# Second layer's modulation: from matmuls in PEER's query loop to GpSimd and ScalarE in the first FFN

## The chip, the cores and the metric

One core of a Trainium2 chip runs the whole kernel. The time is the device time of one execution in microseconds (us); every execution reads its weights from device memory. The engines have the names of the profile: PE (TensorE's matmuls), PEld (its weight loads), DVE (VectorE), ACT (ScalarE), POOL (GpSimd) and SP (SyncE, which here issues most of the loads).

## The reference, cut to what matters

The model is one block with mixers and a PEER layer (product keys and experts), then two layers of a diffusion-style transformer. T = 512 tokens, D = 1024, 256 context tokens, FFN width 22 x 128 = 2816.

```
def second_block(x, c, ctx, c_ctx, w_mod, b_mod, g_attn, g_ffn, ...):
    silu_c = jax.nn.silu(c)
    silu_cc = jax.nn.silu(c_ctx)
    for i in range(2):
        last = i == 1
        mod = silu_c @ w_mod[i] + b_mod[i]          # (1, 6 * 1024)
        mod_c = silu_cc @ w_mod[i] + b_mod[i]
        sh1, sc1, gt1, sh2, sc2, gt2 = jnp.split(mod[:, None, :], 6, axis=-1)
        ...
        h = modulate(rmsnorm(x, g_attn[i]), sh1, sc1)
        hc = modulate(rmsnorm(ctx, g_attn[i]), sh1c, sc1c)
        ...                                          # attention: neighbourhood (0), window (1)
        h = modulate(rmsnorm(x, g_ffn[i]), sh2, sc2)
        x = x + gt2 * conv_ffn(h, ...)
        if not last:
            hc = modulate(rmsnorm(ctx, g_ffn[i]), sh2c, sc2c)
            ctx = ctx + gt2c * conv_ffn(hc, ...)
    return x
```

The change concerns `mod` and `mod_c` of layer 1. They depend on the inputs alone, so they may be computed at any place before layer 1's attention. Of `mod_c` layer 1 uses only the shift and scale of the attention, 2048 of 6144 columns.

## The kernel before, in words

Activations lie transposed (features on partitions). A weight block of 512 KB is loaded by SP's queue (`wload`, three buffers `wraw`) and cut by `split_into` into two parts of a shorter format: ACT writes the high part (`wh`, line 183), DVE the rest (`wl`, line 184); four pairs are kept. PE multiplies three of the four products (lines 206 to 208). The instructions of each engine run in the order in which the build places them, which the engine's own list (the "order" below) shows; waits between engines are semaphores.

In front of the PEER layer's expert loop stand two stages. The query loop has 16 units (8 heads, 2 halves): a unit projects `acc` with `w_query`, copies it (`pq`), takes scores `sc` against the keys (line 863) and DVE searches the 16 largest of each row (`v`, line 843). Two generators are advanced in each unit: `fill(1 + half)` runs steps of `modulation` for layer 1 and `ahead(4)` runs steps of `early_products`, plain f32 matmuls of the first expert blocks (line 814, eight steps for an expert, 28 experts, 224 steps in all). The gate stage ("g_hot") is a pipeline of 96 items on DVE, ACT, POOL and PE (`eb`, `o`, `gps`); in each item `ahead(1 + ...)` runs what is left of the early steps.

`modulation` holds one PSUM bank: 3 groups x 8 blocks x 2 halves load `mraw` (512 KB each) and multiply it with `silc`, the silu of c and c_ctx (line 392).

The first FFN (`conv_ffn(0, True)`) has 11 groups of two j. `up` computes for each j a gate and a value block for the latents (128x512) and the context (128x256): matmuls to `acc`, the convolution on DVE (`cg`, `ca`, lines 1203 to 1205), a silu on ACT (line 1210), the product (line 1215) and its split (`fxh`, `fxl`, `fch`, `fcl`); it also splits the two blocks of `ffn_down` (`fwh`, `fwl`). `down` of the group before runs behind it: matmuls to `pd` (four banks), drained by DVE into XT and CT (line 1254).

`t2` is a pool of five buffers of 128x512 f32. A multiply of that shape on POOL exists in the attention before the FFN (`bias`, line 1355).

Of the kernel before, what the change touches and what calls it, by code (L numbers as in the profile page):

```python
# [10 lines left out]
F32 = mybir.dt.float32  # L11
# [10 lines left out]
D = 1024  # L22
# [85 lines left out]
def body(ctx: ExitStack, tc: tile.TileContext, a: dict, out: bass.AP, dbg=None, stop=None):  # L108
# [10 lines left out]
    def pool(stack, name, bufs=1, **kw):  # L119
        return stack.enter_context(tc.tile_pool(name=name, bufs=bufs, **kw))  # L120
# [256 lines left out]

    tables()

    def modulation(mp_, pmod, ly):  # L380

        bm = cload(mp_, "bmod", [128, 2, 48])
        for g in range(3):
            ps = pmod.tile([128, 512], F32, name="mod")
            for k in range(KT):
                for hf in range(2):

                    raw = mp_.tile([128, 4, 256], F32, name="mraw", bufs=2)
                    sy.dma_start(raw, a["w_mod"][ly, g, k, hf])
                    for c in range(4):  # L390
                        o = 32 * c
                        pe.matmul(ps[o:o + 32, hf * 256:hf * 256 + 256], sc[:, k], raw[:, c],  # L392
                                  start=k == 0 and hf == 0, stop=k == KT - 1 and hf == 1, tile_position=(0, o))
                if k < KT - 1:
                    yield
            rows = mp_.tile([128, 512], F32, name="mrow")
            se.activation(rows, ps, AF.Copy)
            tp = pmod.tile([128, 4, 128], F32, name="mod")
            for b_ in range(4):
                transpose(tp[:, b_], rows[:, b_ * 128:(b_ + 1) * 128])  # L400
            tv = tp.rearrange("p b (c r) -> p c b r", c=4)
            s = slice(g * 16, g * 16 + 16)
            bv = bm[:, ly, s].rearrange("p (c b) -> p c b", c=4)
            for dst, r_ in ((modx, 0), (modc, 1)):
                ve.tensor_tensor(dst[:, ly, s].rearrange("p (c b) -> p c b", c=4), tv[:, :, :, r_], bv, OP.add)
            yield
        for m_, gm in ((modx, gmx), (modc, gmc)):
            for i in range(2):
                ve.scalar_tensor_tensor(gm[:, ly, i * 8:i * 8 + 8], m_[:, ly, i * 24 + 8:i * 24 + 16], 1.0,
                                        c2[:, ly, i * 8:i * 8 + 8], OP.add, OP.mult)  # L410

    def fill(n=1):
        for _ in range(n):
# [355 lines left out]
    with ExitStack() as ex:  # L769
        ep = pool(ex, "peer")  # L770
        pp = ex.enter_context(ExitStack())
        pmod = pool(pp, "pmod", 1, space=PS)
        ph["mix"] = pool(pp, "pmixp", 4, space=PS)
        hh, hl = split_tile("h"), split_tile("l")

        xdr1 = dp.tile([KT, 128, T], F32, name="xdr1")
# [55 lines left out]
                next(early, None)  # L832

        with ExitStack() as gx:
            mp_ = pool(gx, "mod")
            kp_ = pool(gx, "topk")
            ph["mod"] = modulation(mp_, pmod, 1)
            v16 = kp_.tile([128, 4, 16, 16], F32, name="v16")
            i16 = kp_.tile([128, 4, 16, 16], U32, name="i16")
            vc = kp_.tile([128, 4, 8, 16], F32, name="vc")  # L840

            def top16(vals, idx, src, n, tag):
                ve.max(vals[:, 0:8], src)
                ve.max_index(idx[:, 0:8], vals[:, 0:8], src)
                rest = kp_.tile([128, n], F32, name="rest" + tag, bufs=2)
                ve.match_replace(rest, vals[:, 0:8], src, -3.4e38)
                ve.max(vals[:, 8:16], rest)
                ve.max_index(idx[:, 8:16], vals[:, 8:16], rest)

            for hd in range(8):  # L850
                for half in range(2):
                    u = hd * 2 + half
                    keys = kp_.tile([128, 128], F32, name="keys", bufs=2)
                    gp.dma_start(keys, a["keys"][u])
                    ps = acc()
                    proj(ps, wunit(a["w_query"][u]), h)
                    fill(1 + half)
                    ahead(4)
                    q = t2(name="pq")
                    se.activation(q, ps, AF.Copy)  # L860
                    st = mix([128, 4, 128], "sc")
                    for t in range(4):
                        pe.matmul(st[:, t], q[:, t * 128:(t + 1) * 128], keys, start=True, stop=True)
                    for t in range(4):
                        top16(v16[:, t, u], i16[:, t, u], st[:, t], 128, "k")
                for t in range(4):


                    cand = kp_.tile([128, 112], F32, name="cand", bufs=2)
                    for c0, i0, i1, nj in ((0, 0, 4, 16), (64, 4, 16, 4)):  # L870
                        gp.tensor_tensor(cand[:, c0:c0 + (i1 - i0) * nj].rearrange("p (a b) -> p a b", b=nj),
                                         v16[:, t, 2 * hd, i0:i1].unsqueeze(2).to_broadcast([128, i1 - i0, nj]),
                                         v16[:, t, 2 * hd + 1, 0:nj].unsqueeze(1).to_broadcast([128, i1 - i0, nj]), OP.add)
                    top16(vc[:, t, hd], ic[:, t, hd], cand, 112, "c")


            for t in range(4):
                ve.tensor_tensor(vc[:, t, :, 1:], vc[:, t, :, 1:], vc[:, t, :, 0:1].to_broadcast([128, 8, 15]),
                                 OP.subtract)
                ve.memset(vc[:, t, :, 0:1], 0.0)  # L880
            gate = kp_.tile([128, 4, 8, 16], F32, name="gate")
            se.activation(gate, vc, AF.Exp)
            gs = sm.tile([128, 4, 8], F32, name="gs", bufs=1)
            ve.tensor_reduce(gs, gate, AX.X, OP.add)
            ve.reciprocal(gs, gs)
            for t in range(4):
                ve.tensor_tensor(gate[:, t], gate[:, t], gs[:, t].unsqueeze(2).to_broadcast([128, 8, 16]), OP.mult)
            for t in range(4):
                if t == TS:
                    ve.tensor_copy(sgate, gate[:, t].rearrange("p h k -> p (h k)"))  # L890
                else:
                    tps = mix([128, 128], "gtp")
                    transpose(tps, gate[:, t].rearrange("p h k -> p (h k)"))
                    ve.tensor_copy(gT[:, t * 128:(t + 1) * 128], tps)
                ve.tensor_copy(ib16[:, t], i16[:, t])

            htok = rp.tile([128, D], F32, name="tok")
            for i in range(2):
                tps = mix([128, 4, 128], "htp")
                for k in range(4):  # L900
                    transpose(tps[:, k], hf[:, i * 4 + k, ND:])
                se.activation(htok[:, i * 512:i * 512 + 512], tps.rearrange("p k n -> p (k n)"), AF.Copy)
            fill(25)

        with ExitStack() as gx:
            gk = pool(gx, "ghot")
# [68 lines left out]
            def g_sum(it):  # L975
                it["ps"] = mix([128, 4, 128], "gps")
                for ti in range(4):
                    pe.matmul(it["ps"][:, ti], it["o2"][:, ti], it["o1"][:, ti], start=True, stop=True)  # L978
                ahead(1 + (it["q"] % 6 == 5))

            def g_out(it):
                th, tg = it["th"], it["tg"]
# [205 lines left out]
    def conv_ffn(ly, ctx_too):  # L1188
        with ExitStack() as fx:
# [2 lines left out]
            ft = pool(fx, "ft", 6)  # L1192
            ph["acc"] = pool(fx, "facc", 4, space=PS)
            ph["mix"] = pool(fx, "fmix", 4, space=PS)
            cv = cload(fp, "ffn_conv%d" % ly, [128, 4, 44])
            h = normed_x(ly, 1)
            hc = normed_c(fp, ly, 1) if ctx_too else None
# [20 lines left out]
            def up(grp):  # L1218
# [11 lines left out]
                for j in js:  # L1230
                    gs_ = {}
                    for half in (22, 0):
                        u = begun[half + j][0] if begun else wunit(a["ffn_up"][ly, half + j])
                        for i in range(1 if begun else 0, len(parts)):
                            hx, n, tg = parts[i][:3]
                            ps = acc(n=n)
                            proj(ps, u, hx)
                            if half:
                                gs_[i] = gate(ps, n, j)
                            else:  # L1240
                                ys[i].append(gated(ps, n, j, gs_[i], tg))
                        if half and ly == 0 and j == NJ - 1:
                            tables()
                    raw = wload(a["ffn_down"][ly, j], [128, KT, 128])
                    wd.append(split(raw, [128, KT, 128], fw, "fw", 4))
                return ys, wd
# [472 lines left out]
def layout(i):  # L1719
# [32 lines left out]
    for l in range(2):  # L1752
# [7 lines left out]
    o["bmod"] = np.ascontiguousarray(np.stack([colv(i["b_mod_2"][l]) for l in range(2)], 1))  # L1760

    o["w_mod"] = np.ascontiguousarray(
        i["w_mod_2"].reshape(2, KT, 128, 3, 4, 2, 256).transpose(0, 3, 1, 5, 2, 4, 6)).reshape(2, 3, KT, 2, 128, 1024)
    o["ctxT"] = np.ascontiguousarray(i["ctx_2"][0].T)
    o["na_qkv"] = chunks(i["na_w_qkv_2"][0], 256)
    o["na_o"] = units(i["na_w_o_2"][0])
# [31 lines left out]
```

## Time and profile before

| | us |
|---|---|
| median of 3 runs | 3405.89 (3403.52 to 3408.29) |
| profiled execution: time / span | 3405.12 / 3403.4 |
| PE busy | 3278.4 (96%) |
| DVE busy | 2352.6 (69%) |
| ACT busy | 1239.5 (36%) |
| POOL busy | 680.9 (20%) |
| query loop, about | 376 to 558 |
| gate stage, about | 558 to 780 |
| first FFN without its norms, about | 2216 to 2742 |

The span is the profiler's, from the first instruction to the last; the execution's own time is 1.7 us longer. Busy shares are means over stages with different limits, so each stage is read by itself. PE's busy time includes its pipelined ends; a share of 96% says only that PE is rarely without work.

### The profile page before, as it was taken

The numbers are of one execution on the slowest core, as the hardware profiler recorded it, in microseconds if no ns is written. First come the engines' busy times: TensorE is split into PE (matmuls) and PEld (weight loads), VectorE is DVE, ScalarE is ACT, GpSimd is POOL, SyncE is SP. The second block draws the span as 40 slices with busy tenths as digits, with TensorE's granted clock in tenths as the row PEclk, the third lists the DMA queues.
The fourth block names the chain that finished last, engine by engine and source line by source line (L and its number), as shares of the span: only waits on it lengthen the run. The fifth ranks groups of instructions, "written<-read, shape, count | busy, mean of one in ns | idle before, by whom it ended". The sixth has DMA issues, their size and how long they took to land.

```text
span 3403.4 us, 49823 instructions
## 1 busy us (share of the span) xinstructions
PE 3278.4 (96%) x19091; PEld 2762.9 (81%) x19091; DVE 2352.6 (69%) x4718; ACT 1239.5 (36%) x2138; POOL 680.9 (20%) x695
## 2 busy tenths in 40 slices
PE   7889999898999999999999999999999998989999
PEld 5565766677999999999989887888888887878887
DVE  5345678875777777777765557587767778757776
ACT  4134211563333333333354546321221236632221
POOL 0000011564444444444311222000000001100000
PEclk9989999999999999999999999999999999999999
DMA  4535564459888888888832212221111211023331
GB/s 155 196 116 173 176 211 145 165 194 343 296 317 310 307 300 317 305 305 312 287 114 77 72 64 72 68 83 64 67 62 62 62 39 32 14 76 117 94 99 56
DMA packets 151990, 538.07 MB, mean 158 GB/s; under 512 B 17988, under 2 KB 23332, under 8 KB 150216
## 3 DMA queue, kind: packets, MB, share of 16 engines
q1 hardware_dynamic: 97920, 326.76, 28.4%
q0 software_dynamic: 52800, 205.51, 16.9%
q8 instruction: 150, 2.46, 0.3%
q10 hardware_dynamic: 1032, 2.62, 0.2%
q14 instruction: 88, 0.72, 0.1%
HBM read 497.24 MB, written 40.13 MB: 158 GB/s over the span
## 4 chain that ended last, share of the span: by engine, by line
PE 85%; DVE 6%; DMA 3%; issue 2%; ACT 2%; POOL 1%; SPq 0%; POOLq 0%; DVEq 0%; ACTq 0%
PE pv L1100 15%; PE acc L206 11%; PE acc L207 11%; PE acc L208 11%; PE acc L232 9%; PE pd L200 3%; PE pd L199 3%; PE pd L201 3%; PE pt L347 2%; PE acc L814 2%; DMA mraw<-in_w_mod_dram 2%; PE gps L978 1%; PE mod L392 1%; PE on L1400 1%; DVE eb L960 1%
## 5 line engine op out<-in xcount | busy, mean ns | idle before, releaser
L206 PE MATMUL acc<-hh,wh 128*128 128x512 f32 (+1 forms) x1728 | 638.0, 370 | 4.9 <-DVE cg L1205 2.3
L207 PE MATMUL acc<-hl,wh 128*128 128x512 f32 (+1 forms) x1728 | 633.1, 366 | 0.0
L208 PE MATMUL acc<-hh,wl 128*128 128x512 f32 (+1 forms) x1728 | 632.2, 366 | 0.0
L206 PEld LDWEIGHTS acc<-hh,wh 128*128 128x128 f32 x1728 | 326.1, 189 | 51.4 <-issue 8.1
L207 PEld LDWEIGHTS acc<-hl,wh 128*128 128x128 f32 x1728 | 326.1, 189 | 39.4 <-issue 1.2
L208 PEld LDWEIGHTS acc<-hh,wl 128*128 128x128 f32 x1728 | 325.7, 188 | 39.3 <-issue 2.2
L183 ACT ACTIVATE wh<-wraw 128x1024 fp32r<-128x1024 f32 (+1 forms) x189 | 198.9, 1054 | 393.9 <-PE acc L207 168.0
L1100 PE MATMUL pv<-vl,ah 128*128 128x512 f32 x768 | 302.3, 394 | 10.5 <-DVE vl L1080 10.5
L1100 PE MATMUL pv<-vh,al 128*128 128x512 f32 x768 | 302.4, 394 | 0.0
L184 DVE TENSOR_TENSOR wl<-wraw,wh 128x1024 fp32r<-128x1024 f32 (+1 forms) x189 | 230.7, 1222 | 102.3 <-ACT wh L183 98.9
L1100 PE MATMUL pv<-vh,ah 128*128 128x512 f32 x768 | 298.2, 389 | 0.0
L1016 POOL DMA_INDIRECT rows<-in_expert_v_dram,sidx x128 | 191.1, 1493 | 231.5 <-DVE tok L1031 204.6
L1016 POOL DMA_INDIRECT rows<-in_expert_u_rows_dram,sidx x128 | 180.0, 1406 | 229.3 <-DVE rows L1021 217.7
L232 PE MATMUL acc<-wh,hh 128*128 128x256 f32 (+1 forms) x624 | 195.6, 314 | 3.9 <-ACT hh L183 2.3
L232 PE MATMUL acc<-wh,hl 128*128 128x256 f32 (+1 forms) x624 | 193.3, 310 | 0.0
L232 PE MATMUL acc<-wl,hh 128*128 128x256 f32 (+1 forms) x624 | 192.9, 309 | 0.0
L1074 DVE TENSOR_TENSOR al<-ge,ah 128x384 fp32r<-128x384 f32 x128 | 71.3, 557 | 171.7 <-ACT ah L1072 171.2
L1072 ACT ACTIVATE ah<-ge 128x384 fp32r<-128x384 f32 x128 | 67.3, 526 | 328.7 <-PE pv L1100 286.2
L1100 PEld LDWEIGHTS pv<-vl,ah 128*128 128x128 f32 x768 | 144.9, 189 | 39.2 <-DVE vl L1080 10.8
L1100 PEld LDWEIGHTS pv<-vh,al 128*128 128x128 f32 x768 | 145.0, 189 | 30.4
L1021 DVE SCALAR_TENSOR_TENSOR rows<-rows,tok 128x1024 f32<-128x1024 f32 x128 | 154.5, 1218 | 20.1 <-issue 17.4
L1100 PEld LDWEIGHTS pv<-vh,ah 128*128 128x128 f32 x768 | 144.5, 188 | 27.8
(460 smaller groups left out, 7349.4 us busy)
## 6 DMA issues: line engine op xcount, KB each, us to landing
wraw<-in_expert_u_dram SPq DMA_DIRECT2D x128, 512.0 KB, 5.8
vraw<-in_expert_v_dram SPq DMA_DIRECT2D x127, 512.0 KB, 4.8
mraw<-in_w_mod_dram SPq DMA_DIRECT2D x96, 512.0 KB, 4.2
wraw<-in_ffn_up_dram SPq DMA_DIRECT2D x88, 512.0 KB, 3.5
gt<-gdr POOLq DMA_DIRECT2D x31, 768.0 KB, 9.1
wraw<-in_ffn_down_dram SPq DMA_DIRECT2D x44, 512.0 KB, 4.0
gdr<-gst POOLq DMA_DIRECT2D x6, 2048.0 KB, 7.7
gdr<-rows POOLq DMA_DIRECT2D x6, 2048.0 KB, 7.6
```

The costliest lines, as they stand in the source:

```text
L183: se.activation(hi, src, AF.Copy)
L184: ve.tensor_tensor(lo, src, hi.bitcast(F32), OP.subtract)
L199: pe.matmul(ps, wh[i], xh[i], start=i == 0, stop=False)
L200: pe.matmul(ps, wh[i], xl[i], start=False, stop=False)
L201: pe.matmul(ps, wl[i], xh[i], start=False, stop=i == n - 1)
L206: pe.matmul(ps, wh[:, k], hh[:, k], start=k == 0, stop=False)
L207: pe.matmul(ps, wh[:, k], hl[:, k], start=False, stop=False)
L208: pe.matmul(ps, wl[:, k], hh[:, k], start=False, stop=k == KT - 1)
L232: pe.matmul(ps[:, i], x[:, k, s], y, start=k == 0 and i == 0 and x is hh and y is wh, stop=k == KT - 1 and i == nt - 1 and y is wl)
L1016: gp.indirect_dma_start(r, None, src, bass.IndirectOffsetOnAxis(ap=sidx[:, k:k + 1], axis=0))
L1021: pin(ve.scalar_tensor_tensor(r, r, 1.0, htok, OP.mult, OP.mult, accum_out=spre[:, k:k + 1]))
L1100: pe.matmul(sums[t][hf], x[:, s], y[:, d], start=e == 0 and y is vh and x is ah, stop=e == NE - 1 and x is al)
```

## The change

Layer 1's modulation leaves the query loop and its PSUM bank. The new generator `modulation_rows` computes it in the first FFN from the transposed weight: 48 blocks of 128 columns with silu(c), and the first 16 of them again with silu(c_ctx), each block in two halves of 512 inputs, 128 steps in all. A step loads `mrow` [128, 512] (256 KB) by SP's queue; one step later POOL multiplies it by the silu row `crow`, which is the same on all partitions; two steps after that ACT copies it onto itself and sums along the row (`accum_out`). From the second group on, each half of a j advances it by 3 or 4 steps (20 j x 7 = 140 calls for 131 turns). At the end a few small DVE operations add the halves and the bias. In PEER, the bank freed goes to `pmixp` (5 instead of 4), a unit runs `ahead(5)` instead of `ahead(4)`, and a gate item `ahead(1)`.

```
-    def modulation(mp_, pmod, ly):
+    def modulation(mp_, pmod, ly=0):
...
+    def modulation_rows(pl):
+        bm = cload(pl, "bmod", [128, 2, 48])
+        mo = pl.tile([128, 2, 64], F32, name="mo")
+        todo = [(r, b, hf) for r, n in ((0, 48), (1, 16)) for b in range(n) for hf in range(2)]
+        raws, cr = {}, None
+        for s in range(len(todo) + 3):
+            if s < len(todo):
+                r, b, hf = todo[s]
+                raws[s] = t2(512, "mrow")
+                sy.dma_start(raws[s], a["w_mod_rows"][b, :, hf * 512:hf * 512 + 512])
+            if 0 <= s - 1 < len(todo):
+                r, b, hf = todo[s - 1]
+                if b == hf == 0:
+                    cr = pl.tile([128, D], F32, name="crow")
+                    gp.dma_start(cr, a["crow"][r])
+                    se.activation(cr, cr, AF.Silu)
+                gp.tensor_tensor(raws[s - 1], raws[s - 1], cr[:, hf * 512:hf * 512 + 512], OP.mult)
+            if s >= 3:
+                r, b, hf = todo[s - 3]
+                raw, j = raws.pop(s - 3), r * 48 + b
+                se.activation(raw, raw, AF.Copy, accum_out=mo[:, hf, j:j + 1])
+            yield
+        ve.tensor_tensor(mo[:, 0], mo[:, 0], mo[:, 1], OP.add)
+        ve.tensor_tensor(modx[:, 1], mo[:, 0, :48], bm[:, 1], OP.add)
+        ve.tensor_tensor(modc[:, 1, :16], mo[:, 0, 48:], bm[:, 1, :16], OP.add)
+        for i in range(2):
+            scales(modx, gmx, 1, i)
+        scales(modc, gmc, 1, 0)
...
-        pmod = pool(pp, "pmod", 1, space=PS)
-        ph["mix"] = pool(pp, "pmixp", 4, space=PS)
+        ph["mix"] = pool(pp, "pmixp", 5, space=PS)
...
-            ph["mod"] = modulation(mp_, pmod, 1)
...
-                    fill(1 + half)
-                    ahead(4)
+                    ahead(5)
...
-            fill(25)
...
-                ahead(1 + (it["q"] % 6 == 5))
+                ahead(1)
...
+            ph["mod"] = modulation_rows(pool(fx, "fmod")) if ly == 0 else iter(())
...
+                        if grp > 0:
+                            fill(4 if half else 3)
```

PE's list in the query loop before, from the end of one unit to the begin of the next (`sc<-keys,pq` are the scores, `acc<-XT,wraw` early steps):

```order
L392 MATMUL mod<-mraw,silc 32x256 x8
L814 MATMUL acc<-XT,wraw 128x384 x4
L863 MATMUL sc<-keys,pq 128x128 x4
L206 MATMUL acc<-hh,wh 128x512
L207 MATMUL acc<-hl,wh 128x512
L208 MATMUL acc<-hh,wl 128x512
L392 MATMUL mod<-mraw,silc 32x256 x4
```

The same place after the change:

```order
L208 MATMUL acc<-hh,wl 128x512
L849 MATMUL acc<-XT,wraw 128x384 x5
L895 MATMUL sc<-keys,pq 128x128 x4
L206 MATMUL acc<-hh,wh 128x512
L207 MATMUL acc<-hl,wh 128x512
L208 MATMUL acc<-hh,wl 128x512
```

The modulation's matmuls are gone from between the projection and the early steps, of which there are five instead of four.

ACT's list in the first FFN before, for one j, the second of a group (`cg` is the gate's silu, `wh` and `fwh` are weight splits):

```order
L1210 ACTIVATE cg<-cg 128x512
L183 ACTIVATE wh<-wraw 128x1024
L1210 ACTIVATE cg<-cg 128x256
L183 ACTIVATE wh<-wraw 128x1024
L183 ACTIVATE fxh<-ca 128x512
L183 ACTIVATE fch<-ca 128x256
L183 ACTIVATE fwh<-wraw 128x1024 x2
```

The same j after the change (`mrow,mo<-mrow` are the new sums):

```order
L1242 ACTIVATE cg<-cg 128x512
L183 ACTIVATE wh<-wraw 128x1024
L439 ACTIVATE mrow,mo<-mrow 128x512
L1242 ACTIVATE cg<-cg 128x256
L439 ACTIVATE mrow,mo<-mrow 128x512 x6
L183 ACTIVATE wh<-wraw 128x1024
L183 ACTIVATE fxh<-ca 128x512
L439 ACTIVATE mrow,mo<-mrow 128x512 x5
L183 ACTIVATE fch<-ca 128x256
L439 ACTIVATE mrow,mo<-mrow 128x512 x12
L183 ACTIVATE fwh<-wraw 128x1024 x2
```

In this j 24 sums stand between the splits, in a whole group of two j 43; each waits for POOL's multiply of the same buffer.

SP's list in the same part after the change (before, `ffn_up` twice and `ffn_down` once alternate with nothing between):

```order
L188 DMA wraw<-in_ffn_up_dram 128x1024
L428 DMA mrow<-in_w_mod_rows_dram 128x512 x6
L188 DMA wraw<-in_ffn_up_dram 128x1024
L428 DMA mrow<-in_w_mod_rows_dram 128x512 x7
L188 DMA wraw<-in_ffn_down_dram 128x1024
L428 DMA mrow<-in_w_mod_rows_dram 128x512 x7
L188 DMA wraw<-in_ffn_up_dram 128x1024
L428 DMA mrow<-in_w_mod_rows_dram 128x512 x16
```

Weight loads now stand behind `mrow` loads, each of which waits until ACT has freed the buffer that was used five steps before.

## Rows read from the trace of the kernel before

**Rows 1.** Busy time by stretch: its length, then PE, PEld, DVE, ACT, POOL, clock.

```profile
376.00:558.00 182.00, 180.50 (x1032) 120.79 (x1032) 134.50 (x761) 34.23 (x48) 23.46 (x74) 0.99 0.56 191
558.00:780.00 222.00, 201.81 (x1093) 154.40 (x1093) 179.64 (x282) 123.36 (x219) 117.13 (x102) 0.95 0.48 173
2216.00:2742.00 526.00, 525.74 (x3072) 467.07 (x3072) 384.96 (x594) 113.58 (x160) 0.00 (x0) 1.00 0.20 65
```

**Rows 2.** PE's timeline, one head of the query loop (start us, us, what).

```profile
407.26 1.05 PE L863 MATMUL sc<-keys,pq 128*128 128x128 f32 x8
...
413.71 1.07 PE L392 MATMUL mod<-mraw,silc 128*32 128x256 f32 x16
414.71 2.85 PE L814 MATMUL acc<-XT,wraw 128*128 128x384 f32 x8
417.39 1.05 PE L863 MATMUL sc<-keys,pq 128*128 128x128 f32 x8
...
429.70 1.05 PE L863 MATMUL sc<-keys,pq 128*128 128x128 f32 x8
```

**Rows 3.** DVE's waits, 380 to 800 us (total us, times, longest).

```profile
DVE v L843 <- PE sc L863: 38.8, 15, 5.9
```

**Rows 4.** Chain that ended last, 558 to 785 us, shares by line.

```profile
by line: PE acc L814 23.4%; PE gps L978 21.6%; DVE eb L960 13.4%; issue 12.9%; POOL o L972 5.4%; DVE o L972 4.6%; ACT o L970 3.0%; DVE eq L933 1.9%; DVE cu L925 1.8%; DMA wraw<-in_expert_u_dram 1.6%; POOL eq L933 1.4%; SPq L1120 1.3%; DVE e
```

**Rows 5.** ACT's timeline, just before the first FFN's groups.

```profile
2212.09 1.28 ACT L1210 ACT_TABLE_LOAD   x1
```

**Rows 6.** ACT's timeline, first FFN, the first silu of two groups.

```profile
2385.05 0.63 ACT L1210 ACTIVATE cg<-cg 128x512 f32<-128x512 f32 x1 [6.43 <-DVE cg L1205]
...
2434.82 0.63 ACT L1210 ACTIVATE cg<-cg 128x512 f32<-128x512 f32 x1 [6.43 <-DVE cg L1205]
```

**Rows 7.** POOL's multiply at line 1355 (ns: shortest/median/longest).

```profile
L1355 POOL TENSOR_TENSOR bias<-bias,na_mask x32: 1259/1282/2241, 1752.3 to 2112.4; 128x512 f32<-128x512 f32 x32
```

**Rows 8.** ACT's timeline, layer 1's attention, activations with an accumulated sum.

```profile
2829.17 0.73 ACT L352 ACTIVATE sb<-sb,nm 128x513 f32<-128x513 f32 x1
...
2829.89 0.71 ACT L352 ACTIVATE sb<-sb,nm 128x513 f32<-128x513 f32 x1
```

**Rows 9.** DVE by line and shape, 2190 to 2770 us: two SBUF inputs.

```profile
L184 DVE TENSOR_TENSOR wl<-wraw,wh 128x1024 fp32r<-128x1024 f32 x46 | 55.9, 1216 | 0.4 <-ACT wh L183 0.4
...
L184 DVE TENSOR_TENSOR fwl<-wraw,fwh 128x1024 fp32r<-128x1024 f32 x22 | 26.1, 1221 | 1.9 <-ACT fwh L183 0.7
...
L1215 DVE TENSOR_TENSOR ca<-ca,cg 128x512 f32<-128x512 f32 x22 | 15.1, 692 | 0.8
L184 DVE TENSOR_TENSOR fxl<-ca,fxh 128x512 fp32r<-128x512 f32 x22 | 15.0, 685 | 0.0
...
L184 DVE TENSOR_TENSOR fcl<-ca,fch 128x256 fp32r<-128x256 f32 x22 | 9.2, 420 | 4.9 <-ACT fch L183 4.8
L1215 DVE TENSOR_TENSOR ca<-ca,cg 128x256 f32<-128x256 f32 x22 | 9.2, 419 | 0.3
```

**Rows 10.** Timeline in the attention, a POOL multiply beside a DVE split.

```profile
1834.19 1.23 DVE L184 TENSOR_TENSOR wl<-wraw,wh 128x1024 fp32r<-128x1024 f32 x1 [1.08 <-ACT wh L183]
...
1834.39 2.18 POOL L1355 TENSOR_TENSOR bias<-bias,na_mask 128x512 f32<-128x512 f32 x1 [1.70 <-DMA bias<-in_na_bias_dram]
```

**Rows 11.** Timelines, gate stage and attention: DVE beside POOL.

```profile
606.75 5.83 DVE L972 TENSOR_TENSOR o<-eb,gT 128x512 f32<-128x512 bf16 x1
...
607.18 3.84 POOL L933 TENSOR_TENSOR eq<-eq,ib 128x2048 bf16<-128x2048 bf16 x1
...
610.98 1.05 POOL L972 TENSOR_TENSOR o<-eb,gT 128x512 f32<-128x512 bf16 x1
...
2063.33 0.48 DVE L357 TENSOR_SCALAR sb<-sb,den 128x512 f32<-128x512 f32 x1
...
2063.58 1.37 POOL L1355 TENSOR_TENSOR bias<-bias,na_mask 128x512 f32<-128x512 f32 x1 [2.41 <-DMA bias<-in_na_bias_dram]
...
2063.91 1.33 DVE L357 TENSOR_SCALAR sb<-sb,den 128x512 f32<-128x512 f32 x1
```

More of the change, by code (lines that the diff above doesn't have):

```diff
@@ L388, in modulation @@
                     raw = mp_.tile([128, 4, 256], F32, name="mraw", bufs=2)
-                    sy.dma_start(raw, a["w_mod"][ly, g, k, hf])
+                    sy.dma_start(raw, a["w_mod"][g, k, hf])
                     for c in range(4):
@@ L408, in modulation, with scales @@
             for i in range(2):
-                ve.scalar_tensor_tensor(gm[:, ly, i * 8:i * 8 + 8], m_[:, ly, i * 24 + 8:i * 24 + 16], 1.0,
-                                        c2[:, ly, i * 8:i * 8 + 8], OP.add, OP.mult)
+                scales(m_, gm, ly, i)
+    def scales(m_, gm, ly, i):
+        ve.scalar_tensor_tensor(gm[:, ly, i * 8:i * 8 + 8], m_[:, ly, i * 24 + 8:i * 24 + 16], 1.0,
+                                c2[:, ly, i * 8:i * 8 + 8], OP.add, OP.mult)
+    def modulation_rows(pl):
[26 more added lines that the diff above has]
+        scales(modc, gmc, 1, 0)
     def fill(n=1):
@@ L834, in body @@
         with ExitStack() as gx:
-            mp_ = pool(gx, "mod")
             kp_ = pool(gx, "topk")
-            ph["mod"] = modulation(mp_, pmod, 1)
             v16 = kp_.tile([128, 4, 16, 16], F32, name="v16")
@@ L1762, in layout @@
     o["w_mod"] = np.ascontiguousarray(
-        i["w_mod_2"].reshape(2, KT, 128, 3, 4, 2, 256).transpose(0, 3, 1, 5, 2, 4, 6)).reshape(2, 3, KT, 2, 128, 1024)
+        i["w_mod_2"][0].reshape(KT, 128, 3, 4, 2, 256).transpose(2, 0, 4, 1, 3, 5)).reshape(3, KT, 2, 128, 1024)
+    o["w_mod_rows"] = np.ascontiguousarray(i["w_mod_2"][1].T).reshape(48, 128, D)
+    o["crow"] = np.ascontiguousarray(np.broadcast_to(np.stack([i["c_2"][0], i["c_ctx_2"]])[:, None], (2, 128, D)))
     o["ctxT"] = np.ascontiguousarray(i["ctx_2"][0].T)
```

## The prediction

> **What bounds the kernel now.** I read the busy time by stretch first [rows 1]. Its columns give, for each stretch, how long each engine worked. The change touches three stretches. In the query loop (376 to 558 us) PE is busy for 180.5 of 182.0 us. In the gate stage (558 to 780 us) nobody is full: PE 201.8 and DVE 179.6 of 222 us. In the first FFN (2216 to 2742 us) PE is busy for 525.74 of 526.00 us, DVE for 385.0, ACT for 113.6 and GpSimd for nothing. So what leaves PE in the query loop is worth its full time, in the gate stage only a part of it, and in the FFN the new work costs nothing as long as it never makes PE wait. The whole question is whether GpSimd, ACT and SP can carry 128 steps there without PE noticing.
>
> **Query loop.** On PE's timeline one head (two units) runs from the score matmuls at 407.26 to those at 429.70: 22.44 us [rows 2]. Its first unit lasts to 417.39, so 10.13 us, and holds one fill: modulation matmuls from 413.71 to 414.71, 1.00 us. Without it the unit is 9.13 us. The second unit has two fills and lasts 12.31 us, so its fills cost 3.18 us, more than 2 x 1.00: some matmuls there wait for their weights. After the change a unit has no fill and one early step more. Four steps stand from 414.71 to 417.39, 2.68 us, so one is 0.67 us. A unit becomes 9.13 + 0.67 = 9.80 us and a head 19.60, a gain of 2.84; for eight heads **-22.7 us**. Bounds: if the weight waits of the second unit come back as another wait, 24 fills at 1.00 less 16 steps at 0.67 is -13.3; if the small idle around the fills goes too, -26. DVE does not take over as the limit here: it waited 38.8 us in 15 times for the scores [rows 3], 2.6 us each, and a unit gets shorter by only 1.4 us on average.
>
> **Gate stage.** The 16 steps taken into the query loop are missing here: 16 x 0.67 = 10.7 us of PE. The chain that ended last in this stretch gives the early products 23.4%, the gate matmuls 21.6%, the rest to DVE, GpSimd and issue [rows 4], so between nothing and all of the 10.7 can be gained. I take 0.4 of it, nearer to the 23% than to the whole: **-4 us**.
>
> **Norms of the FFN.** The silu of the two context rows (`crow`) stands on ACT just ahead of the two small norm activations of each of the FFN's two norms, so four activation tables more are loaded. One load is 1.28 us [rows 5]. Two of them can lie in waits; I charge the other two, 2 x 1.28 = **+2.6 us** (bounds 1 and 5). Nothing else is in their way.
>
> **The 128 steps in the FFN.** First their rate. By the order the steps are not spread over the 20 j at which they are written: ACT has 43 of them in each group of two j, so they are through in 128/43 = 2.98 groups. A group takes 49.8 us now, from silu 2385.05 to silu 2434.82 [rows 6]. A GpSimd multiply of the very shape, 128x512 f32, takes 1.28 us [rows 7], so 43 of them take 55.0 us, more than the group. ACT adds 43 steps of 0.72 us, the pitch of two activations with an accumulated sum [rows 8]: 31.0 us beside some 11 that it works in a group now (113.6 of 526 us), which fits. So GpSimd becomes the slowest engine of these three groups, and ACT waits for it step by step, in order, with the weight splits (`wh`, `fwh`) and the silu queued behind. SP is tied in too: each `mrow` load waits for ACT to free one of five buffers, and the next weight load stands behind it in the same queue. DVE's `wl` waits for `wh`, and behind `wl` stand the drains of the `pd` banks, without which PE can't go on.
>
> Second, what GpSimd and DVE do to each other. The FFN's DVE work with two SBUF inputs is, in one group, four `wl` and two `fwl` at 1.22 us, two each of `ca` at 0.69 and 0.42 and of `fxl` and `fcl` at 0.69 and 0.42: 14 operations, 4 x 1.22 + 2 x 1.22 + 4 x 0.69 + 4 x 0.42 = 11.8 us [rows 9]. In the trace such operations and GpSimd's exclude each other. A multiply that began 0.20 us after a `wl` of 1.23 us took 2.18 us instead of 1.28, and the `wl` lost nothing [rows 10]. And a DVE operation that came first to a busy GpSimd took 5.83 us, over two GpSimd operations of 3.84 and 1.05 us that ran one after the other; in f32, beside a multiply of this shape, a DVE operation of 0.48 us took 1.33 [rows 11]. So the first cost is GpSimd's: 55.0 + 11.8 = 66.8 us a group instead of 49.8, +17.0. The second is DVE's: it meets a GpSimd that is nearly always in a multiply and waits on average half of one, 0.64 us, 14 times: +9.0. I count both, since what is late at DVE is `wl`, and so the weights, the drains and then the loads that feed GpSimd again. A group is then 75.8 us, +26.0, and 2.98 groups make **+77.5 us**.
>
> The Trainium skill, GPSIMD Engine Reference, section 1 (Specifications), says that GpSimd's way to SBUF is shared with VectorE, with contention where a DVE instruction has two SBUF inputs or runs in a mode on both ports; the two rows above agree with it. Its introduction calls the engine the wrong choice for ordinary elementwise arithmetic, which speaks against this change.
>
> Bounds of this term: if the port costs nothing, 43 x 1.28 = 55.0, so 5.2 x 2.98 = +15.5 us; if PE's stock of split weights and free banks swallows even that lag, 0; if every one of the 14 operations waits for a whole multiply, 55.0 + 11.8 + 14 x 1.28 = 84.7, so 34.9 x 2.98 = +104 us. I stay between these because the two overlaps of the trace show both directions of the wait.
>
> **The sum.** The profiled execution took 3405.1 us, 1.7 above its span of 3403.4 and 0.8 below the median of 3405.89. 3405.1 - 22.7 - 4 + 2.6 + 77.5 = **3458.5 us**, forecast 3458 (+1.5%). The later stages see the same operations as before; layer 1 needs its modulation only after the FFN, when the steps have long ended.
>
> **The rivals.**
> *The port costs only its own time.* DVE's waits are covered by its slack (385.0 of 526 us), and a group is 66.8 us: +50.7 instead of +77.5, 3432 us. For it speaks that DVE is idle a quarter of the time; against, that what waits is in front of PE's weights. Chance 0.20.
> *Other side: the multiplies don't collide.* If GpSimd and DVE hardly lose to each other in the FFN's mix (the 32 multiplies of the trace have a median of 1.28 us and a shortest of 1.26, so most met nothing, and few lie beside `wl`), the cost is 0 to 15.5 us and the gain of 26.7 in the peer stage wins: 3381 to 3397 us. It decides from the point where a group costs less than (22.7 + 4 - 2.6)/2.98 = 8.1 us more, that is, below 57.9 us. Against it stand the stretched multiply of 2.18 us, and 43 x 1.28 > 49.8. Chance 0.13.
> *DVE is starved.* Five buffered multiplies one after the other hold DVE as in the row of 5.83 us; each of the 14 operations waits for a whole multiply or longer: +104 us, 3485, and more where it is two. Chance 0.14.
> *The steps do not pack* and spread over more groups, so that less than 49.8 us of GpSimd falls in each: then the cost nearly vanishes and the result is near no change, 3400 to 3410. The order speaks against it. Chance 0.03.
> The likeliest, my sum, keeps 0.50, with its own range of 3440 to 3480.
>
> **How the numbers follow.** About 0.2% (7 us) can be told from no change here. Below 3399 lies the other-side case, 0.13, between 3399 and 3413 the last one with 0.03, above it all else, 0.84. The range must leave out no more than 0.2: from 3395 it leaves out most of the other-side case (0.10), to 3500 the worst of the starved case (0.07).
>
> **What the changed profile would show.** Query loop: a head of about 19.6 us on PE, with five early steps together and no modulation. First FFN: three groups of 65 to 85 us, the other eight at 49.8; GpSimd busy 190 us or more there (multiplies longer than 1.28 us); DVE's `wl`, `fwl`, `ca` and `fxl` with a mean above their 1.22 and 0.69 in these groups; and PE waiting at `pd` and `acc` for DVE, with ACT's `wh` behind `mrow` steps that wait for GpSimd. Wrong would make it: multiplies that keep 1.28 us beside DVE, a landing of the 256 KB loads so slow that SP and not GpSimd sets the step, or PE without idle time in the FFN.

## The result, and the profile after

The changed kernel takes 3450.23 us (median of 4 runs, 3442.31 to 3451.12) against 3406.09 of the kernel before: ratio 1.0127, 95% interval 1.0113 to 1.0141. It is slower by 44 us; 3458 was forecast, inside a range of 3395 to 3500. The profiled execution took 3449.96 us.

The busy time by stretch, columns as in [rows 1] (behind the clock stand DMA's busy share and GB/s); the first two stretches are the query loop and the gate stage, which now end earlier, the last two the first FFN's groups with steps and those without:

```profile
376.00:540.00 164.00, 163.72 (x696) 121.01 (x695) 133.25 (x772) 32.04 (x46) 25.61 (x79) 0.99 0.26 81
540.00:780.00 240.00, 199.78 (x1107) 153.15 (x1106) 188.46 (x269) 126.89 (x224) 124.80 (x106) 0.97 0.52 195
...
2198.00:2429.00 231.00, 178.49 (x991) 155.69 (x990) 165.56 (x199) 124.06 (x306) 173.52 (x125) 0.88 0.61 195
2429.00:2790.00 361.00, 359.10 (x2080) 318.23 (x2079) 257.65 (x400) 74.73 (x107) 1.64 (x3) 1.00 0.19 61
```

PE, which was full in the FFN, is busy for 178 of the first 231 us and full again after them. GpSimd works 174 of those 231 us. So the loss lies where the steps are.

How far it goes is read from three lines of the code that both kernels have: the scores (first and last start), the last expert matmul, and the last drain of CT, which ends the first FFN. Before:

```profile
L863 PE MATMUL sc<-keys,pq x128: 272/275/378, 390.3 to 554.2; 128*128 128x128 f32 x128
L1100 PE MATMUL pv<-vh,ah x768: 387/389/560, 786.0 to 1739.5; 128*128 128x512 f32 x192
L1254 DVE SCALAR_TENSOR_TENSOR CT<-pd,modc,CT x88: 474/484/486, 2272.5 to 2742.1; 128x256 f32<-128x256 f32 x88
```

After:

```profile
L895 PE MATMUL sc<-keys,pq x128: 272/275/377, 387.4 to 533.3; 128*128 128x128 f32 x128
L1131 PE MATMUL pv<-vh,ah x768: 387/389/397, 760.2 to 1713.3; 128*128 128x512 f32 x192
L1288 DVE SCALAR_TENSOR_TENSOR CT<-pd,modc,CT x88: 477/485/487, 2270.7 to 2786.0; 128x256 f32<-128x256 f32 x88
```

The query loop from the first score to the last goes from 163.9 to 145.9 us (-18.0), from there to the first expert matmul from 231.8 to 226.9 (-4.9). What I call the FFN stage from here on, from the last `pv` start to the last drain of CT, goes from 1002.6 to 1072.7 us (**+70.1**). It begins before the first layer's attention, so that all that reaches into the norms is in it.

ACT's timeline, the first silu of the groups, which answers to [rows 6]:

```profile
2198.20 1.16 ACT L1242 ACTIVATE cg<-cg 128x512 f32<-128x512 f32 x2
2225.41 0.63 ACT L1242 ACTIVATE cg<-cg 128x512 f32<-128x512 f32 x1
...
2290.45 0.63 ACT L1242 ACTIVATE cg<-cg 128x512 f32<-128x512 f32 x1 [3.80 <-DVE cg L1237]
...
2365.93 0.62 ACT L1242 ACTIVATE cg<-cg 128x512 f32<-128x512 f32 x1
...
2428.92 0.63 ACT L1242 ACTIVATE cg<-cg 128x512 f32<-128x512 f32 x1 [6.37 <-DVE cg L1237]
...
2478.75 0.63 ACT L1242 ACTIVATE cg<-cg 128x512 f32<-128x512 f32 x1 [6.43 <-DVE cg L1237]
```

Three groups take 65.0, 75.5 and 63.0 us, the next one 49.8 as before. Before, the first of the three took 47.1 and the others 49.8 each, and the 27.2 us ahead of them took 22.3 (ACT's timeline before; the next first silu is at 2335.29):

```profile
2216.14 1.29 ACT L1210 ACTIVATE cg<-cg 128x512 f32<-128x512 f32 x2 [2.77 <-DVE cg L1205]
...
2238.47 0.61 ACT L1210 ACTIVATE cg<-cg 128x512 f32<-128x512 f32 x1
...
2285.52 0.63 ACT L1210 ACTIVATE cg<-cg 128x512 f32<-128x512 f32 x1 [6.43 <-DVE cg L1205]
```

The four differences, 4.9, 18.0, 25.7 and 13.2 us, make 61.8. GpSimd's multiply, and DVE's operations with two SBUF inputs by shape (2190 to 2790 us), answer to [rows 7] and [rows 9]:

```profile
L435 POOL TENSOR_TENSOR mrow<-mrow,crow x128: 1258/1307/2301, 2191.1 to 2408.8; 128x512 f32<-128x512 f32 x128
```

```profile
L184 DVE TENSOR_TENSOR wl<-wraw,wh 128x1024 fp32r<-128x1024 f32 x44 | 72.2, 1640 | 27.1 <-ACT wh L183 27.1
...
L184 DVE TENSOR_TENSOR fwl<-wraw,fwh 128x1024 fp32r<-128x1024 f32 x20 | 29.5, 1511 | 9.9 <-ACT fwh L183 9.0
L184 DVE TENSOR_TENSOR fxl<-ca,fxh 128x512 fp32r<-128x512 f32 x22 | 21.7, 986 | 0.1
L1247 DVE TENSOR_TENSOR ca<-ca,cg 128x512 f32<-128x512 f32 x22 | 20.1, 918 | 0.7
```

Each mean is above that of before, over eleven groups of which under four are touched: the collisions are there, (1.640 - 1.216) x 44 = 18.7 us for `wl` alone and some 41 us for the six kinds of [rows 9] together. DVE's drains of `pd`, which read PSUM, keep their time (XT 747 ns in both kernels).

Who waits, in the same stretch: PE for DVE's drains of `pd` and for its convolution (before, PE waits for nothing from 2220 to 2740 us), ACT's sums for GpSimd, and in SP's queue (SPq) the `mrow` loads (line 428) for ACT's sums. DVE in turn waits for ACT's splits: the row of `wl` above has 27.1 us for `wh`, against 0.4 before.

```profile
PE pd L199 <- DVE XT L1288: 39.6, 3, 14.5
PE acc L206 <- DVE ca L1237: 11.3, 2, 8.1
```

```profile
ACT mrow L439 <- POOL mrow L435: 78.5, 97, 4.5
```

```profile
SPq L428 <- ACT mrow L439: 93.1, 83, 4.6
```

The chain of work that ended last, 2160 to 2480 us, runs through GpSimd's multiplies and the landing of their loads; in the kernel before, PE's matmuls to `acc` and `pd` are 87% of the chain in this window:

```profile
by line: POOL mrow L435 16.8%; DMA mrow<-in_w_mod_rows_dram 16.2%; issue 10.6%; PE acc L206 6.4%; PE acc L207 6.3%; PE acc L208 6.2%; DVE wl L184 5.6%; ACT mrow L439 4.3%; PE pd L199 3.3%; PE pd L200 3.2%; PE pd L201 3.2%; ACT wh L183 2.4%;
```

### The profile page after: what moved, and what is told of

It is laid out like the page before. It is cut to its first block, busy times and chain, and to the rows that moved or that the text cites. A ratio compares the mean times of both kernels' runs of the same rounds, so it can differ in the third digit from the quotient of the medians.

```text
span 3448.2 us, 49677 instructions
## 1 busy us (share of the span) xinstructions
PE 3254.8 (94%) x18695; PEld 2757.3 (80%) x18695; DVE 2396.6 (70%) x4714; ACT 1330.4 (39%) x2398; POOL 864.1 (25%) x825
## 4 chain that ended last, share of the span: by engine, by line
PE 65%; DVE 5%; DMA 2%; issue 2%; POOL 2%; ACT 2%; SPq 0%; POOLq 0%; DVEq 0%; ACTq 0%
PE pv L1131 15%; PE acc L206 9%; PE acc L208 9%; PE acc L207 9%; PE acc L232 7%; PE pd L199 3%; PE pd L200 3%; PE pd L201 3%; PE pt L347 2%; POOL mrow L435 2%; DMA mrow<-in_w_mod_rows_dram 1%; PE on L1434 1%; PE mix L232 1%; DVE wl L184 1%; PE s L1395 1%
## 5 line engine op out<-in xcount | busy, mean ns | idle before, releaser
L184 DVE TENSOR_TENSOR wl<-wraw,wh 128x1024 fp32r<-128x1024 f32 (+1 forms) x189 | 249.5, 1322 | 125.4 <-ACT wh L183 121.9
L435 POOL TENSOR_TENSOR mrow<-mrow,crow 128x512 f32<-128x512 f32 x128 | 179.3, 1441 | 65.2 <-DMA mrow<-in_w_mod_rows_dram 58.4
L199 PE MATMUL pd<-fxh,fwh 128*128 128x512 f32 x352 | 139.9, 399 | 39.6 <-DVE XT L1288 39.6
L1131 PEld LDWEIGHTS pv<-vl,ah 128*128 128x128 f32 x768 | 144.8, 189 | 39.6 <-DVE vl L1111 11.3
```

The source lines that it names most:

```text
L184: ve.tensor_tensor(lo, src, hi.bitcast(F32), OP.subtract)
L199: pe.matmul(ps, wh[i], xh[i], start=i == 0, stop=False)
L435: gp.tensor_tensor(raws[s - 1], raws[s - 1], cr[:, hf * 512:hf * 512 + 512], OP.mult)
L1131: pe.matmul(sums[t][hf], x[:, s], y[:, d], start=e == 0 and y is vh and x is ah, stop=e == NE - 1 and x is al)
```

## The experiments

Two theories were held against each other. **Port:** GpSimd's rate and its collisions with DVE make the cost by themselves. **Queues:** the steps cost because others stand behind them, weight loads behind `mrow` loads on SP, splits behind sums on ACT. Every kernel is the changed one with the edit shown. The FFN stage is worked out as above from each run's profile, one execution each. In these profiles the first score starts anywhere from 384.5 to 397.6 us, which the stage leaves out, so it can differ by some us from what the medians say.

| kernel | median us | ratio to before, 95% | FFN stage, us | against before |
|---|---|---|---|---|
| changed | 3450.23 | 1.0127 (1.0113 to 1.0141) | 1072.7 | +70.1 |
| no steps | 3385.1 | 0.9944 (0.9925 to 0.9963) | 1004.2 | +1.6 |
| no multiply | 3408.76 | 1.002 (1.0007 to 1.0033) | 1026.4 | +23.8 |
| half multiply | 3420.21 | 1.0046 (1.003 to 1.0063) | 1040.4 | +37.8 |
| multiplies alone, two rows | 3497.49 | 1.028 (1.0254 to 1.0306) | 1117.4 | +114.8 |
| multiplies alone, one row | 3390.61 | 0.9954 (0.9937 to 0.9971) | 1007.7 | +5.1 |
| no sums | 3438.63 | 1.0104 (1.0083 to 1.0125) | 1059.0 | +56.4 |
| loads on ACT's queue | 3401.25 | 0.9989 (0.9979 to 1.0) | 1020.5 | +17.9 |
| loads and sums spread | 3393.94 | 0.9968 (0.9956 to 0.998) | 1016.5 | +13.9 |
| loads alone spread | 3405.45 | 1.0002 (0.999 to 1.0013) | 1024.3 | +21.7 |
| spread, silu later | 3389.25 | 0.9949 (0.9932 to 0.9965) | 1009.2 | +6.6 |
| spread on DVE, silu later | 3387.95 | 0.9942 (0.9926 to 0.9959) | 1007.1 | +4.5 |
| silu later alone | 3443.58 | 1.0111 (1.0092 to 1.013) | 1061.7 | +59.1 |

**No steps.**

```
-        todo = [...]; the loop over the steps
+        ve.memset(mo, 0.0)
+        yield
```

> The changed kernel without its 128 steps: no loads, multiplies or sums, layer 1's modulation is the bias alone. What is left of the change is the peer stage. Theory (the sum of the prediction): the peer stage gains 26.7 us and nothing else changes, so 3406 - 27 = 3379 us, and the first FFN's groups are 49.8 us again. Rival (the gain in the peer stage is partly given back later, or the extra activation tables and not the steps cost time): 3385 to 3400 us.

3385.1 us, so 0.56% under before, 19 us (13 to 26 by the interval), less than the 27 expected: at the lower end of the rival's range, not at the theory's 3379. In its profile the first score starts at 395.3, the last expert matmul at 1720.7: 1325.4 us against 1349.2 before, 23.8 less, nearly the 23.3 of the changed kernel. The gain of the peer stage stands, and is kept.

**No multiply.**

```
-                gp.tensor_tensor(raws[s - 1], raws[s - 1], cr[...], OP.mult)
```

> The changed kernel without GpSimd's 128 multiplies; the loads on SP's queue and the sums on ACT stay, in nearly the same order, so the sums are of the unmultiplied weights. Port theory (GpSimd's rate and its lock against DVE make the cost, SP and ACT only pass it on): a step takes ACT's 0.72 us, 43 steps 31 us beside some 11 us of other work, which fits in 49.8 us, so within 8 us of the kernel without steps: 3380 to 3388. Queue theory (weight loads that stand behind mrow loads, splits that stand behind sums): more than half of the 70 us stays, 3415 to 3450.

3408.76: between both. PE's wait for the drains is 11.5 us instead of 39.6:

```profile
PE pd L199 <- DVE XT L1287: 11.5, 3, 4.6
```

Loads and sums alone, packed as they are, cost about a third of the 70 us; the rest needs GpSimd.

**Multiplies alone.**

```
-                raws[s] = t2(512, "mrow")
-                sy.dma_start(raws[s], ...)
+                raws[s] = own                    # one tile, set once
...
-                gp.tensor_tensor(raws[s - 1], raws[s - 1], cr[...], OP.mult)
+                gp.tensor_tensor(own, own, cr[...], OP.mult)
...
-                se.activation(raw, raw, AF.Copy, accum_out=mo[:, hf, j:j + 1])
```

> The changed kernel with GpSimd's 128 multiplies alone: on a tile of their own that nobody loads, sums or waits for, so they run one after the other from the begin of the FFN, 96 and 32; layer 1's modulation is the bias alone. Port theory: DVE's two-input operations wait for multiplies as in the changed kernel (there they are 41 us longer in all) while the multiplies last, 128 x 1.3 to 1.5 us, and PE loses 20 to 50 us at pd and acc: 3400 to 3430. If DVE waits until GpSimd has nothing more to do, the first operation waits for over 100 us and the time is 3480 or more. Queue theory: nobody waits for GpSimd, so 3380 to 3385.

3497.49 us looks like the starving case, but isn't. ACT's timeline has the cause, the second load of `crow`, which GpSimd issues behind 96 multiplies; ACT stands at its silu, and with it the norms:

```profile
2259.95 1.28 ACT L436 ACT_TABLE_LOAD   x1 [86.92 <-DMA crow<-in_crow_dram]
```

The run tells nothing of the port. It was made again with one row (`if s == 1` for the load, the product of `crow` with itself into `own`, the silu kept behind the gates of the second group):

> GpSimd's 128 multiplies alone once more, now without the second crow load that stood behind 96 of them, and with the one silu kept behind the first gates on ACT, so the multiplies run one after the other from the second group on, where the changed kernel has them. They write a tile that nobody reads; no mrow loads, no sums, modulation is the bias alone. Port theory: DVE's 14 two-input operations of a group each wait for 0.6 to 1.3 us, DVE goes from 36 to 45 to 54 us in a group of 49.8 for about 4 groups, so 0 to 25 us over the kernel without steps: 3385 to 3410. Starving (DVE waits until GpSimd pauses): over 100 us more, 3490. Queue theory (only the ties to SP and ACT cost): 3380 to 3387.

3390.61 us: inside the range that was set for the port theory (3385 to 3410), near its lower end, and 3.6 above the queue theory's. The multiplies stand one after the other from 2223.20 to 2408.27, 49 of them in the 70.89 us shown, and DVE's operations are longer, yet PE hardly waits:

```profile
2229.56 70.89 POOL L436 TENSOR_TENSOR own<-crow 128x512 f32<-128x512 f32 x49
```

```profile
L184 DVE TENSOR_TENSOR wl<-wraw,wh 128x1024 fp32r<-128x1024 f32 x53 | 68.2, 1286 | 4.3 <-ACT wh L183 4.3
...
L184 DVE TENSOR_TENSOR fwl<-wraw,fwh 128x1024 fp32r<-128x1024 f32 x22 | 30.1, 1399 | 1.2
L184 DVE TENSOR_TENSOR fxl<-ca,fxh 128x512 fp32r<-128x512 f32 x22 | 23.2, 1061 | 0.0
L1247 DVE TENSOR_TENSOR ca<-ca,cg 128x512 f32<-128x512 f32 x22 | 21.1, 964 | 0.8
```

```profile
PE pd L199 <- DVE XT L1288: 2.6, 4, 0.9
```

`fxl` loses (1.061 - 0.685) x 22 = 8.3 us, more than in the changed kernel, but `wl` only some 3.6 us against 18.7; the six kinds together are some 26 us longer, against 41. The stage is 3.5 us longer than without steps. Collisions of this size cost little: DVE's slack takes them. The port theory in its strong form, in which they make the 70 us, falls; a small cost of theirs stays, and the long waits of `wl` in the changed kernel are not made again here.

**Half the multiply.**

```
-                gp.tensor_tensor(raws[s - 1], raws[s - 1], cr[:, hf * 512:hf * 512 + 512], OP.mult)
+                gp.tensor_tensor(raws[s - 1][:, :256], raws[s - 1][:, :256], cr[:, hf * 512:hf * 512 + 256], OP.mult)
```

> The changed kernel with each multiply over 256 of the 512 columns (the other half is summed unmultiplied); loads, sums and order as in the changed kernel. Rate theory (43 multiplies take longer than a group): 43 x 0.66 = 28 us fit, so it falls to the level without multiplies, 3409, plus a small toll: 3406 to 3420. Rival (each meeting of GpSimd and DVE costs, so the count decides): 3440 to 3450.

3420.21, 0.2 above the upper end of the rate theory's range and 20 below the rival's. With a multiply of 0, 0.74 and 1.31 us the stage costs 23.8, 37.8 and 70.1 us: it goes with GpSimd's time for a step, and steeper in the second half.

**No sums, and loads on another queue.** Which queue passes GpSimd's pace on? In the first kernel ACT has nothing of the steps (`raws.pop(s - 3)` is all that is left of the sum), in the second the load is issued by ACT (`se.dma_start` for `sy.dma_start`).

> The changed kernel without ACT's 128 sums (modulation is the bias alone); the loads on SP's queue and GpSimd's multiplies stay and are packed as before, and a load now waits for the multiply that used its buffer five steps earlier. SP tie: weight loads still stand behind mrow loads that come at GpSimd's pace, 43 x 1.4 = 60 us for a group of 49.8, so 3425 to 3450. ACT tie: with nothing of the steps on ACT the splits are free, and 3390 to 3410 is left.

> The changed kernel, all work done, with the mrow loads issued by ACT's queue instead of SP's; the steps are packed as before, some 40 in a group. ACT itself frees the buffer that a load waits for, and weight loads no longer stand behind mrow loads. SP tie (the groups wait because weights are loaded late behind mrow loads): most of the FFN's 70 us goes, 3390 to 3415. ACT tie (weight splits and silus stand behind sums that wait for GpSimd, 43 x 1.4 = 60 us a group): it stays, 3435 to 3455.

3438.63 and 3401.25: both as the SP tie wants it. Without sums, SP's `mrow` loads wait for GpSimd, and ACT waits for weights, which it did not in the changed kernel:

```profile
SPq L429 <- POOL mrow L436: 125.0, 116, 9.6
```

```profile
ACT wh L183 <- DMA wraw<-in_ffn_up_dram: 41.8, 7, 15.1
```

```profile
PE pd L199 <- DVE XT L1288: 37.4, 3, 15.9
```

Against the multiplies alone (+5.1) this kernel adds the loads on SP and the earlier silu, and has +56.4. DVE's six kinds are some 31 us longer here, little more than the 26 of the multiplies alone, so the collisions don't make the difference. The second kernel loads the same bytes in the same part of the program, so it isn't the transfers that cost. It is no clean opposite, though: its multiplies begin from 2193.2 to 2430.9, 20 us longer than in the changed kernel, over more groups, so it is also less dense.

**Spread.** The loads, or loads and sums, are kept behind what the program wrote before them on their engine, so that a group has 14 steps.

```
-                sy.dma_start(raws[s], a["w_mod_rows"][...])
+                pin(sy.dma_start(raws[s], a["w_mod_rows"][...]))
...
-                se.activation(raw, raw, AF.Copy, accum_out=...)
+                pin(se.activation(raw, raw, AF.Copy, accum_out=...))
```

> The changed kernel with all its work, but each mrow load and each sum kept behind what was written before it on SP and ACT, so that every j has 7 steps and every group of two j 14 instead of 43. Theory (the density makes the cost: 43 x 1.28 us is more than a group's 49.8): 14 x 1.28 = 18 us a group leave GpSimd idle for 60%, a DVE operation meets a multiply one time in three, and PE keeps its groups of 50 to 51 us: 3383 to 3395 us. Rival (each step costs the same wherever it stands, 0.54 us a step): 3440 to 3450.

3393.94 us, faster than both kernels, with all work done and multiplies that last longer than in the changed kernel:

```profile
L435 POOL TENSOR_TENSOR mrow<-mrow,crow 128x512 f32<-128x512 f32 x128 | 189.4, 1507 | 304.3 <-DMA mrow<-in_w_mod_rows_dram 293.2 <-ACT cg L1242 5.3 <-ACT crow L434 4.6
```

```profile
PE pd L199 <- DVE XT L1288: 2.0, 3, 1.5
```

With the loads alone:

> The changed kernel, all work done, with one edit: only the mrow loads are kept behind what was written before them on SP's queue (7 for each j); multiplies and sums follow freely, silu and tables stay in the norms. SP tie: this alone removes the waits of the weight loads, so it equals the spread kernel, 3390 to 3398, and its stage from the last expert matmul to the last drain of CT is 1012 to 1018 us. Rival (the sums on ACT have to be spread as well): 3405 or more.

3405.45, a miss: the rival was right by a hair. 48 of the 70 us go with the one edit, but the sums are left where they wait for GpSimd (179.3 us in all, against 5.2 with the sums spread too), and some of the drains with them:

```profile
ACT mrow L439 <- POOL mrow L435: 179.3, 80, 7.0
```

```profile
PE pd L199 <- DVE XT L1288: 10.5, 6, 6.3
```

**Silu later.**

```
-                    se.activation(cr, cr, AF.Silu)
+                    pin(se.activation(cr, cr, AF.Silu))
```

On top of the spread:

> The spread kernel (7 steps in each j) with crow's silu kept behind the gates of the second group on ACT, so that it forces no activation table in the FFN's norms. All work is done. In the spread kernel 8.7 of the 12 us that are left against the kernel without steps lie before the first drain of pd. Theory (tables and silu in the norms, and the first steps): 5 to 9 us less than the spread kernel, 3385 to 3390. Rival (what is left is DVE's waiting in the groups): no change, 3392 to 3396.

3389.25, as expected. The intervals of this kernel and of the spread one overlap, but in the profiles the part from the last `pv` to the first silu of the FFN goes from 484.4 to 476.7 us. With the product and the sum in one DVE operation instead of GpSimd and ACT, beside that:

```
+                pin(ve.scalar_tensor_tensor(raw, raw, 1.0, crs[r][...], OP.mult, OP.mult, accum_out=mo[:, hf, j:j + 1]))
```

> The same with the product and the sum of a step in one DVE operation instead of GpSimd's multiply and ACT's sum. All work is done. At the 1.22 us that DVE takes for two SBUF inputs of 128x1024, a step is about 0.7 us, 14 in a group 9.8 us; DVE goes from 36.5 to 46.3 us of 49.8. If DVE's slack carries it: 3383 to 3392. Rival (drains and splits come late behind the steps): 3400 to 3420.

3387.95, not to be told from the one before it. A step is short on DVE:

```profile
L439 DVE SCALAR_TENSOR_TENSOR mrow<-mrow,crow x128: 679/685/696, 2230.7 to 2685.4; 128x512 f32<-128x512 f32 x128
```

The introduction of the Trainium skill's GPSIMD Engine Reference calls VectorE roughly twice as fast for elementwise work; 0.685 us with the sum against 1.31 for the multiply alone agrees. And with the silu alone:

> The changed kernel, all work done, with one edit: crow's silu is kept behind the gates of the second group on ACT, so no activation table is loaded for it in the norms; the steps start later and stay packed. If the tables in the norms cost what the spread kernels showed, it is 5 to 9 us faster than the changed kernel's 3450: 3441 to 3445. Rival (the steps that started in the norms gave that back, since they filled the wait for the first group): 3448 to 3455.

3443.58: 6.7 us under the changed kernel, with intervals that overlap. In the profiles the part from the last `pv` to the first silu goes from 484.9 to 477.0 us, and of the five activation tables that the changed kernel loads more than before, from 2111.86 to 2181.46, none is left. So the silu ahead of the norms costs 7 to 8 us.

## Why the prediction was right, point by point

**Query loop, -22.7 forecast, -18.0 measured.** A unit after the change is 145.9/15 = 9.73 us, forecast 9.80: right. A unit before is 163.9/15 = 10.93 us on average; the head that I took from [rows 2] has 22.44/2 = 11.22. One head stood for eight, and it was a slow one; and the measured part holds 15 units, where the forecast counted 16.

**Gate stage, -4 forecast, -4.9 measured.** Right.

**Norms, +2.6 forecast.** Too small. From the last `pv` to the first silu of the FFN it is 476.6 us before (to 2216.14) and 484.9 after (to 2198.20), +8.3, and with the silu pinned 477.0 (the pin gives 6.7 us back in the median and 11.0 in the profiled stage). The tables were miscounted: five more, one of them for the silu itself, 6.4 us in all. That two of four lie in waits was a guess, and no run bears it out.

**The steps, +77.5 forecast, +61.8 measured** (70.1 less 8.3). The groups of 65.0, 75.5 and 63.0 us average 67.8; 75.8 was forecast, 66.8 without DVE's waits. PE stands idle for 52.5 of these 231 us; the rest of the 61.8 is, by an estimate, matmuls at the lower clock (last section). The rate is confirmed: 128 multiplies from 2191.1 to 2410.1 (the last begins at 2408.8), 1.71 us a step, where 75.8/43 = 1.76 was forecast. Its make-up was not: GpSimd was busy with the multiplies for 179.3 us, 1.40 a step (1.55 forecast; the mean of one is 1.44), and the rest is GpSimd waiting, mostly for its loads. That the two make the forecast rate is luck.

**The mechanism.** The step of the prediction that failed is "I count both", the 9.0 us a group for DVE's waits that should reach PE. In the changed kernel DVE did wait, and the drains did come late, but the collisions are not the main reason: multiplies packed more tightly, with nobody tied to them, make some 26 of the 41 us by which DVE's operations are longer, and cost 3.5 us. The rival that DVE's slack covers its waits was right on this point, though its 3432 is 18 us too low, and single operations did wait for several multiplies (last section). GpSimd's own loss was put too high as well: 43 x (1.44 - 1.28) = 6.9 us a group instead of 11.8. One reading went too far: the operation of 1.33 us in [rows 11] has one tensor input, so it is no example of those with two. The rule of the Trainium skill (GPSIMD Engine Reference, section 1, Specifications) that GpSimd and VectorE contend for SBUF where a DVE instruction has two SBUF inputs agrees with the longer operations here; it did not decide the time.

What the runs put in its place is the tie, which the prediction had named but not priced: 43 steps at GpSimd's pace are more than a group, and PE's weights pass through queues that keep the pace of the steps. In the changed kernel DVE waits for ACT's splits, which stand behind sums, and ACT waits for no weight load; without the sums ACT waits 41.8 us for weight loads. SP alone is enough for most of it (no sums: +56.4; the same multiplies without loads: +5.1); with the steps thinned to 14 a group the tie has slack, and the collisions, longer than before, cost little. The two parts don't add: 23.8 without multiplies and 5.1 without ties make 29, not 70. That is what a queue does when its members turn slower than what stands behind them needs.

**The sum.** Against the forecast the query loop is 4.7 us worse, the norms 5.7 worse, the gate stage 0.9 and the steps 15.7 better. Errors of 27 us leave 6, so that 3450 lies within 8 us of 3458 is in part luck.

**Open.** Which of the two queues ends PE's waits is not settled: with the loads off SP and the sums still on ACT the stage has only +17.9, but at a lower density. What ACT's sums cost alone at the same packing was not isolated; the difference between the changed kernel and that without sums (13.7 us) and between the two spread kernels (7.8 us) bound it loosely. Why the last half of the multiply costs more than the first is argued (43 x 0.74 us fit into the group's 49.8, 43 x 1.31 don't), not shown.

## What to carry to other kernels

Work for an idle engine is not free because that engine is idle: count its steps per period of the bound engine in the order that was built, not in the order that was written, and compare with the period. Here 43 x 1.3 us stood in 49.8, and the two pins that brought 14 made the same work cheap. Loads of a side task don't belong in front of the main task's loads in one queue unless the side task is faster than the main one, and a load that stands behind 96 multiplies in GpSimd's queue can stop a norm for 87 us.

## What the runs showed of the hardware

A single DVE operation can wait for more than one multiply: in the changed kernel two `fwl` together took 6.78 us instead of 2.44, and a `wl` 6.74 instead of 1.22 (DVE's timeline, then GpSimd's):

```profile
2281.34 6.78 DVE L184 TENSOR_TENSOR fwl<-wraw,fwh 128x1024 fp32r<-128x1024 f32 x2 [5.12 <-ACT fwh L183]
...
2306.24 6.74 DVE L184 TENSOR_TENSOR wl<-wraw,wh 128x1024 fp32r<-128x1024 f32 x1 [8.22 <-ACT wh L183]
```

```profile
2255.27 30.63 POOL L435 TENSOR_TENSOR mrow<-mrow,crow 128x512 f32<-128x512 f32 x23 [0.78 <-ACT mrow L439]
2295.20 16.70 POOL L435 TENSOR_TENSOR mrow<-mrow,crow 128x512 f32<-128x512 f32 x13 [9.30 <-DMA mrow<-in_w_mod_rows_dram]
```

The rows of multiplies end at 2285.90 and 2311.90, and the DVE operations 2.2 and 1.1 us after that, about their own time. Yet with 128 multiplies in a row `fwl`, `ca` and `fxl` lost 0.18 to 0.38 us in the mean (multiplies alone, one row). What decides which of the two happens was not found.

After its wait of 14.5 us PE's first matmuls ran at the lower of the two clocks (the granted clock is 0.51 from 2252 to 2260 us, in the wait, 0.64 from 2260 to 2268 and 1.00 in the next 8 us, so 1.2 GHz and then 2.4): from 2263.44 on they are 0.63 us long and 0.43 apart, from 2266.15 on 0.39 long and 0.23 apart (PE's timeline):

```profile
2262.84 0.80 PE L199 MATMUL pd<-fxh,fwh 128*128 128x512 f32 x1 [14.50 <-DVE XT L1288]
2263.44 0.63 PE L200 MATMUL pd<-fxl,fwh 128*128 128x512 f32 x1
...
2266.15 0.39 PE L201 MATMUL pd<-fxh,fwl 128*128 128x512 f32 x1
```

Six or seven matmuls at 0.2 us more each are some 1.3 us. After the two other long waits for drains thirteen matmuls each ran so (granted clock 0.50 from 2332 to 2340 and from 2404 to 2412 us), and ten around 2380 us:

```profile
2335.42 0.79 PE L199 MATMUL pd<-fxh,fwh 128*128 128x512 f32 x1 [11.55 <-DVE XT L1288]
...
2406.78 0.79 PE L199 MATMUL pd<-fxh,fwh 128*128 128x512 f32 x1 [13.57 <-DVE XT L1288]
```

That makes some 43 matmuls and, as an estimate, 9 us of the 61.8, beside the 52.5 in which PE stands idle.
